# A two-layer decoder trunk: the second layer's input projection by seven products of block sums

## The chip, the cores and the metric

The kernel runs on one core of one Trainium2 chip. The metric is device time in microseconds (us). The time before is the median of three runs, 1857.2 us (1854.56 to 1858.99).

## The reference

The input x is 1024 tokens by 1024 features (h below). There are two layers. Each normalizes h, multiplies it with an input matrix, mixes, attends to a memory of 256 tokens, gates, and adds the product with an output matrix to h:

```python
hn = rms_norm(h, ln_g[i])
# layer 0: differential attention          # layer 1: causal pooling, windows 2, 4, 8, 16
proj = einsum('bsd,de->bse', hn, w_in)      # layer 0: 1024 x 7168, layer 1: 1024 x 4096
u, q_mem, gate = split(proj)                # layer 1: 1536 + 512 + 2048 columns
y = diff_attention(u, ...) or multiscale_pool(u, w_group, scale)
m = memory_attention(q_mem, mem_n, w_kv[i])
z = concatenate([y, m]) * silu(gate)
h = h + einsum('bse,ed->bsd', z, w_out[i])  # w_out: 2048 x 1024
```

After both layers h is normalized once more. `multiscale_pool` takes for each of four groups of 384 columns the mean of the last 2, 4, 8 or 16 tokens, subtracts the token itself, and multiplies with a 384 x 384 matrix.

## The kernel before, in words

Everything is kept with features on the 128 partitions and tokens along the free axis; the 1024 tokens are two halves of 512, worked on in the order 1, 0. A float32 product is made of three matmuls: each operand is split into a rounded part and a rest (a cast on ScalarE, and a subtract on VectorE or GpSimd), and `mm3` (L118) issues high x high, high x rest, rest x high. A tile of 128 output features for one half of the tokens is 8 such triples, one for each 128 input features (`project`, L204): 24 matmuls of 128 x 512.

The activations of a layer are split once, before normalization: `new_hidden` (L500) makes `hh` and `hl` from h times the gain. The row scale of the normalization is not known yet then. `row_means` and `row_spread` (L526, L532) make it, and each projected tile is multiplied by it when it is read from its PSUM bank, with the table `rsb` (L605, L625, L817, L1143).

TensorE's order is written by hand. Jobs are put in a list by `plan` (L971); `run_jobs` (L164) issues the loads of the next job (weights over the SP queue, then their split) before it runs the present one, and yields after each triple or so ("a step"). Attention and memory units play their own matmuls in between at given step counts (`play`, L747; `mem_units`, L703, with a list of starts). On the other engines the order comes from a planner with a priority by place in the program. PSUM has two banks of the tag "pj" for projections, two "t", three "s" and one "o".

The stages: attention of layer 0 with its projections; memory keys and values of both layers, and eight units of memory attention for layer 0 (`other_layers`, L1202), the last of which play into the next stage; the output projection of layer 0 (`out_jobs`, L1232), here called out0; the input projection of layer 1 with the layer's memory attention, the pooling and the group products, here the mixing stage; the output projection of layer 1 (out1).

out0 goes half by half in three rounds of 2, 4 and 2 output tiles. A round reads all 16 z tiles of its half from DRAM again: a chunk is one 512 KB weight tile with four z tiles (rounds 0 and 2) or two (round 1), 24 matmuls each way. `operand` (L1250) loads z into a raw tile `zf` (`nf` = 5 of them), casts into `zr` (`nz` = 6) and subtracts. `finish` (L1305) adds the residual to a finished tile, squares it, stores h to DRAM, and calls `new_hidden`. The row means of half 1 are taken after the first chunk of half 0, the spread after the third.

In the mixing stage, `projection_pair` (L181) runs two query tiles for half 1 while the row scale of half 0 is made; each further `projection` (L172) loads a weight tile of 512 KB, splits it, and runs both halves. `pooled_evac` (L1131) makes the sliding sums on GpSimd by doubling (L1155), subtracts the token and splits. `group_job` (L1175) runs one of a group's three output tiles in two "pj" banks, 9 matmuls a half, and multiplies with scale and gate (L1191). Groups go 0, 1, 2, 3. Layer 1's z tiles 12 to 15 are read first by out1, then 0 to 11.

## Time and profile before

| what | value |
|---|---|
| median of three runs | 1857.2 us (1854.56 to 1858.99) |
| profiled execution, own time | 1851.84 us |
| its span, first to last instruction | 1850.1 us |
| TensorE busy | 1778.2 us (96%), 8670 matmuls |
| VectorE, ScalarE, GpSimd busy | 66%, 49%, 39% |
| granted TensorE clock, mean | 0.989 |

A row of the waits reads: engine, tile and line that waited, what it waited for, us in total, times, longest. A row of a group of instructions reads: line, engine, operation, tiles, shapes, count, busy us, mean ns, and idle time ahead of them. In a row of one line's instructions three numbers behind the count are the shortest, median and longest duration in ns. A matmul's row has its start and a modelled duration; matmuls overlap, so the distance of two starts is what one costs.

### The profile page before, as it was taken

Reading aid. Unit: us, or ns where it says so; the run is one execution under the profiler, and the core shown is the slowest. Engines: PE = TensorE matmul, PEld = TensorE weight load, DVE = VectorE, ACT = ScalarE, POOL = GpSimd, SP = SyncE. Lnnn points to the kernel's source line nnn. Section 1 sums busy time; section 2 is a strip of 40 time slices with the busy share of each in tenths; the row PEclk is TensorE's granted clock in tenths of the full one; section 3 lists DMA queues with packets and bytes.
Section 4 is the critical chain, followed back from the end, with each engine's and each line's share of the span. In section 5 each row is a group of like instructions: output and inputs, shape, how many; then the busy total and the mean of one; then the engine's idle time right before and its main releaser. Section 6 shows DMA issues by size and latency. Waiting matters only on the chain. (4 is left out here: it accounts for less than half of the span.)

```text
span 1850.1 us, 24825 instructions
## 1 busy us (share of the span) xinstructions
PE 1778.2 (96%) x8670; PEld 1479.3 (80%) x8670; DVE 1223.2 (66%) x2446; ACT 899.7 (49%) x1649; POOL 724.1 (39%) x618
## 2 busy tenths in 40 slices
PE   6899999999999999999999999999999999999997
PEld 5788888888888888888787877778887777878885
DVE  7778788888889888876557777635453435444413
ACT  6667657657657756743256555533321111124522
POOL 4434344444344434433254343432332444513452
PEclk9999999999999999999999999999999999999998
DMA  5001111111111111112454778632213122155542
GB/s 184 27 31 58 46 42 51 46 47 51 41 52 52 40 53 46 58 58 69 169 184 172 246 258 277 216 106 86 92 37 96 47 73 77 56 161 200 172 148 97
DMA packets 80956, 186.04 MB, mean 101 GB/s; under 512 B 9120, under 2 KB 17024, under 8 KB 80832
## 3 DMA queue, kind: packets, MB, share of 16 engines
q1 hardware_dynamic: 79440, 182.04, 29.5%
q10 hardware_dynamic: 1296, 2.17, 0.3%
q8 instruction: 68, 1.11, 0.3%
q14 instruction: 56, 0.46, 0.1%
q0 software_dynamic: 96, 0.26, 0.1%
HBM read 152.67 MB, written 31.77 MB: 100 GB/s over the span
## 5 line engine op out<-in xcount | busy, mean ns | idle before, releaser
L865 ACT ACTIVATE e<-e,st 128x640 f32<-128x640 f32 (+4 forms) x192 | 148.2, 773 | 109.9 <-DVE st L856 108.8
L115 POOL TENSOR_TENSOR wl_o<-wf_o,wh_o 128x384 fp32r<-128x384 f32 x64 | 97.5, 1523 | 216.0 <-ACT wh_o L112 205.7
L877 POOL TENSOR_SCALAR e<-e,st 128x640 f32<-128x640 f32 (+4 forms) x96 | 76.3, 795 | 198.0 <-DVE st L876 115.5
L1267 DVE TENSOR_TENSOR zr<-zf,zr 128x512 fp32r<-128x512 f32 x132 | 114.5, 886 | 27.0 <-ACT zr L1266 26.7
L115 DVE TENSOR_TENSOR wl_o<-wf_o,wh_o 128x640 fp32r<-128x640 f32 x64 | 58.2, 909 | 110.5 <-ACT wh_o L112 104.7
L112 ACT CAST wh_o<-wf_o 128x1024 fp32r<-128x1024 f32 x64 | 67.2, 1049 | 115.7 <-PE ob L122 70.9
L905 ACT CAST wth<-wt 128x512 fp32r<-128x512 f32 (+2 forms) x168 | 72.4, 431 | 103.5 <-PE wt L902 73.8
L856 DVE CUSTOM_DVE_ANT_0 e<-s,mask 128x512 f32<-128x512 f32 (+2 forms) x192 | 109.3, 580 | 12.3 <-PE s L851 10.8
L1266 ACT CAST zr<-zf 128x512 fp32r<-128x512 f32 x132 | 80.8, 618 | 67.2 <-DMA zf<-z 32.9
L121 PE MATMUL ga<-hh,wh_ga 128*128 128x512 f32 x256 | 104.0, 406 | 3.5 <-DVE mqf L625 3.5
L121 PE MATMUL pga<-hh,wh_pga 128*128 128x512 f32 x256 | 100.5, 392 | 6.5 <-DVE pz L1191 4.6
L123 PE MATMUL ga<-hh,wl_ga 128*128 128x512 f32 x256 | 101.4, 396 | 0.0
L122 PE MATMUL ga<-hl,wh_ga 128*128 128x512 f32 x256 | 101.1, 395 | 0.0
L122 PE MATMUL ob<-zr,wh_o 128*128 128x512 f32 x256 | 100.3, 392 | 0.0
L121 PE MATMUL ob<-zr,wh_o 128*128 128x512 f32 x256 | 100.3, 392 | 0.0
L123 PE MATMUL ob<-zr,wl_o 128*128 128x512 f32 x256 | 100.3, 392 | 0.0
L122 PE MATMUL pga<-hl,wh_pga 128*128 128x512 f32 x256 | 99.8, 390 | 0.0
L123 PE MATMUL pga<-hh,wl_pga 128*128 128x512 f32 x256 | 99.7, 389 | 0.0
L851 PE MATMUL s<-kb,qa 128*128 128x512 f32 (+2 forms) x288 | 98.5, 349 | 0.9 <-DVE kb L803 0.9
L851 PE MATMUL s<-kb,qlo 128*128 128x512 f32 (+2 forms) x288 | 98.4, 349 | 0.0
L121 PE MATMUL k<-hh,wh_k 128*128 128x512 f32 x192 | 79.2, 412 | 8.5 <-ACT wh_k L112 8.5
L906 DVE TENSOR_TENSOR wtl<-wt,wth 128x512 fp32r<-128x512 f32 (+2 forms) x168 | 82.7, 492 | 6.0 <-ACT wth L905 4.8
(285 smaller groups left out, 5547.6 us busy)
## 6 DMA issues: line engine op xcount, KB each, us to landing
zf<-z SPq DMA_DIRECT2D x132, 256.0 KB, 3.8
wf_o<-in_w_out SPq DMA_DIRECT2D x64, 512.0 KB, 3.4
wf_ga<-in_w_in SPq DMA_DIRECT2D x16, 512.0 KB
wf_pga<-in_w_in SPq DMA_DIRECT2D x16, 512.0 KB, 4.4
wf_q<-in_w_in SPq DMA_DIRECT2D x12, 512.0 KB, 3.1
wf_v<-in_w_in SPq DMA_DIRECT2D x12, 512.0 KB, 3.8
z<-rs SPq DMA_DIRECT2D x24, 256.0 KB, 3.2
z<-z SPq DMA_DIRECT2D x24, 256.0 KB, 2.0
```

The costliest lines, as they stand in the source:

```text
L115: eng.tensor_tensor(wl[:, c], wf[:, c], wh[:, c].bitcast(F32), op=ALU.subtract)
L121: nc.tensor.matmul(out, sh, mh, start=first, stop=False)
L122: nc.tensor.matmul(out, sh, ml, start=False, stop=False)
L123: nc.tensor.matmul(out, sl, mh, start=False, stop=last)
L851: nc.tensor.matmul(sc[m][:, w], q[half][part][:, m, qs], k[kh][:, m, w], start=(part == 0), stop=(part == 1),)
L856: nc.vector.tensor_tensor_reduce(out=es[m][:, lo:hi], in0=sc[m][:, : hi - lo], in1=self.mask[:, S - n + lo : S - n + hi], scale=1.0, scala ...
L865: nc.scalar.activation(es[m][:, :n], es[m][:, :n], AF.Exp, bias=least[m], scale=-1.0, accum_out=st[:, 2, m : m + 1],)
L877: nc.gpsimd.tensor_scalar(es[1][:, :n], es[1][:, :n], st[:, 3, 1:2], 1.0, op0=ALU.mult, op1=ALU.mult)
L905: nc.scalar.copy(wh[:, lo:hi], t[:, lo:hi])
L906: nc.vector.tensor_tensor(wl[:, lo:hi], t[:, lo:hi], wh[:, lo:hi].bitcast(F32), op=ALU.subtract)
L1266: nc.scalar.copy(z[:, 0, :], zf)
L1267: nc.vector.tensor_tensor(z[:, 1, :], zf, z[:, 0, :].bitcast(F32), op=ALU.subtract)
```

## The change

The projection of layer 1 is done in blocks of halves. The input features are cut in two (block rows of the weights: a[:, k0], a[:, k1] and b[:, k0], b[:, k1] for a pair of output tiles a, b), and so are the tokens (X11, X21 for half 1, X12, X22 for half 0). Two output tiles for two halves are 8 block products; seven products of sums and differences of blocks give the same (Winograd's form), each of 4 triples, that is 12 matmuls. Its parts:

- The activations are normalized first: `finish` of layer 0 keeps h in SBUF in place of splitting it. When a half's row scale is spread, `scale_hidden` multiplies the 8 tiles by gain and scale on VectorE. `blocks_first` splits half 1 (inside out0's half 0, after the third chunk); `blocks_second` makes the four sums T1 to T4 and splits them and X22, after out0. Evacuations need no scale any more.
- `product` loads a pair's two weight tiles, makes S1, S2, S3 and the difference in place on VectorE, splits the block in a box (`split_box`), and runs 12 matmuls. Boxes are prepared four entries ahead (`entry`), raw tiles up to four more. `done` combines products on VectorE from their banks; products 4 and 3 add up in the banks of 7 and 5.
- The first four pairs (memory query and its gate) run products 1 and 2, which need half 1 alone, one pair after the other; row means and spread of half 0 stand behind the first and the second of them. Their loads of the first tile are made twice.
- The groups go 3, 2, 1, 0, with all six output tiles of a group in six banks ("t", "t", "s", "s", "s", "o"), one input tile after the other; w_group is stored in another order.
- The sliding sums go to VectorE from the second doubling on; buffers of the pooling shrink.
- The memory attention of layer 0 ends before out0 starts (starts 94 to 138 in place of 100 to 150); layer 1's units get other starts and single buffers.
- SBUF for the blocks comes from smaller buffers: in out0 `nf` 5 to 3, `nz` 6 to 5, one square tile; mask and rope tables live with the attention, `rsb` up to the end of layer 0's memory attention.

```diff
-        self.projection_pair([mq1(0), mq1(1)], lambda: means0(0), lambda: spread0(0))
-        self.mark("out0")
...
+        firsts = [self.pair(mq1(m), gate1(NH + m)) for m in range(MH)]
+        for i, p in enumerate(firsts):
+            self.product(p, 1)
+            self.product(p, 2)
+            if i == 0:
+                self.between(lambda: means0(0))
+            if i == 1:
+                self.between(lambda: spread0(0))
+        self.mark("out0")
+        for p in firsts:
+            for n in (6, 7, 5, 4, 3):
+                self.product(p, n)
...
+        def pairs(a, b):
+            p = self.pair(a, b)
+            for n in (1, 6, 2, 7, 5, 4, 3):
+                self.product(p, n)
+
+        for gi in (3, 2, 1, 0):
+            t = 3 * gi
+            pairs(u1(t), u1(t + 1))
...
+            pairs(gate1(t), u1(t + 2))
+            self.group(gi, 0)
+            pairs(gate1(t + 1), gate1(t + 2))
+            self.group(gi, 1)
+            self.group(gi, 2)
...
+        def prep(box):
+            a, b = (p["a0"], None) if early else (p["a"], p["b"])
+            if n == 6:
...
+                nc.vector.tensor_tensor(p["s1"], b[:, k0], b[:, k1], op=ALU.add)
+                nc.vector.tensor_tensor(p["s2"], p["s1"], a[:, k0], op=ALU.subtract)
+            if n == 7:
+                nc.vector.tensor_tensor(a[:, k0], a[:, k0], b[:, k0], op=ALU.subtract)
+            if n == 3:
+                nc.vector.tensor_tensor(p["s2"], a[:, k1], p["s2"], op=ALU.subtract)
...
+            self.split_box(box, f, HALF, nc.vector if n in (6, 3, 5) else nc.gpsimd)
...
+        def done(out):
+            if n == 1:
+                keep("p1", out)
+            elif n == 2:
+                evac0(1, out, None)
+            elif n == 6:
+                keep("u2", out, p["p1"])
+            elif n == 7:
+                keep("u3", out, p["u2"])
+            elif n == 5:
+                evac1(0, out, p["u3"])
+            elif n == 4:
+                evac1(1, out, p["u2"])
+            else:
+                evac0(0, out, p["u2"])
...
+    def scale_hidden(self, half, bc):
+        g = self.ln_g[1]
+        for d in self.h_order(half):
+            f = self.hid[half, d]
+            self.nc.vector.scalar_tensor_tensor(
+                f, f, g[:, d : d + 1], bc, op0=ALU.mult, op1=ALU.mult
+            )
+            yield d, f
...
+    def blocks_first(self, bc):
+        nc = self.nc
+        for d, f in self.scale_hidden(1, bc):
+            name, i = ("11", d) if d < 4 else ("21", d - 4)
+            self.split_block(name, i, f, 2 * d, 2 * d + 1, (nc.vector, nc.gpsimd)[d % 2])
+
+    def blocks_second(self, bc):
...
+            nc.vector.tensor_tensor(x11, x12, x11, op=ALU.subtract)
+            nc.vector.tensor_tensor(t2, x22, x11, op=ALU.subtract)
+            self.split_block("t2", i, t2, 16 + 2 * i, 17 + 2 * i, (nc.gpsimd, nc.vector)[i % 2])
+            nc.gpsimd.tensor_tensor(x21, x21, t2, op=ALU.subtract)
+            nc.gpsimd.tensor_tensor(x12, x22, x12, op=ALU.subtract)
...
-                nc.gpsimd.tensor_tensor(
+                (nc.gpsimd if sh == 1 else nc.vector).tensor_tensor(
...
-        nf, nz = ((5, 6), (4, 20))[layer]
+        nf, nz = ((3, 5), (4, 20))[layer]
...
             if layer == 0:
                 nc.sync.dma_start(self.h_dram[d][:, cols], h)
-                self.new_hidden(half, d, h, self.ln_g[1])
...
-                self.keep_spread(half)
+                bc = self.opool.tile([P, HALF], F32, tag="bc", name=f"bc{half}")
+                (self.blocks_second, self.blocks_first)[half](self.keep_spread(half, bc))
```

More of the change, by code (lines that the diff above doesn't have):

```diff
@@ L80, in build @@
             self.stream = self.run_jobs()
-            self.attention_layer()
+            with tc.tile_pool(name="scale", bufs=1, reuse_waits="tile") as pool:
+                self.rsb = pool.tile([P, S], F32, name="rsb")
+                self.attention_layer()
+                self.memory_layer()
             self.other_layers()
@@ L628, in mem_query_evac, with mem_query @@
         return evac
-    def mem_query(self, pool, layer, m, half):
+    def mem_query(self, pool, layer, m, half, bufs):
         nc = self.nc
@@ L701, in mem_value, with mem_units @@
         nc.tensor.matmul(o, kv[:, 0, c], wl, start=False, stop=(j == 1))
-    def mem_units(self, pool, layer, gates, starts):
+    def mem_units(self, pool, layer, gates, starts, bufs=2):
         nc = self.nc
@@ new lines, in pair, with entry, load @@
+    def pair(self, first, second):
+        return {"specs": (first, second)}
+    def entry(self, prep, run, fetch=lambda: None):
+        n = len(self.entries)
+        self.entries.append((prep, fetch))
+        boxes = {}
+        def load():
+            while self.ready < min(n + 4, len(self.entries)):
+                i = self.ready
+                self.ready += 1
+                for j in range(i, min(i + 4, len(self.entries))):
+                    self.entries[j][1]()
+                pool, tag = (
+                    (self.wpool, "wh"), (self.wpool, "wl"), (self.spool, "wb")
+                )[i // 2 % 3]
+                box = pool.tile(
+                    [P, 2, HALF], F32R, tag=tag, **({"bufs": 2} if tag == "wb" else {}),
+                    name=f"box{i}",
+                )
+                self.entries[i][0](box)
+                self.box[i] = box
+            return self.box.pop(n)
+        self.jobs.append((load, run))
@@ new lines, in land, with mem_query_keep, evac @@
+    def land(self, t, bank, more):
+        if more is None:
+            self.nc.scalar.copy(t, bank)
+        else:
+            self.nc.vector.tensor_tensor(t, bank, more, op=ALU.add)
+    def mem_query_keep(self, m):
+        def evac(half, bank, more):
+            f = self.epool.tile([P, HALF], F32, tag="ev", bufs=6, name=f"mqf1{m}{half}")
+            self.land(f, bank, more)
+            self.nc.sync.dma_start(self.mq_dram[1][m][:, half * HALF : (half + 1) * HALF], f)
+        return evac
@@ new lines, in gate_keep, with evac @@
+    def gate_keep(self, t):
+        nc = self.nc
+        def evac(half, bank, more):
+            pool, bufs = (self.mpool, 2) if t >= NH else (self.xpool, 3)
+            g = pool.tile([P, HALF], F32, tag=f"gate{half}", bufs=bufs, name=f"gap{t}{half}")
+            th = pool.tile([P, HALF], F32, tag="tanh", name=f"tanhp{t}{half}")
+            if more is not None:
+                self.land(g, bank, more)
+            x = bank if more is None else g
+            nc.scalar.activation(th, x, AF.Tanh, scale=0.5)
+            nc.vector.scalar_tensor_tensor(g, th, 1.0, x, op0=ALU.add, op1=ALU.mult)
+            self.gates[1][t][half] = g
+        return evac
@@ new lines, in slot, with split_block @@
+    def slot(self, j, name, dtype=F32R):
+        if j < 32:
+            half, d, part = 1 - j // 16, j % 16 // 2, "hl"[j % 2]
+            return self.hpool.tile([P, HALF], dtype, tag=f"h{part}{half}{d}", name=name)
+        return self.h2pool.tile([P, HALF], dtype, tag=f"n{j - 32}", name=name)
+    def split_block(self, name, i, f, hi, lo, by):
+        h = self.slot(hi, f"x{name}h{i}")
+        l = self.slot(lo, f"x{name}l{i}")
+        self.nc.scalar.copy(h, f)
+        by.tensor_tensor(l, f, h.bitcast(F32), op=ALU.subtract)
+        self.X.setdefault(name, {})[i] = (h, l)
@@ L1313, in finish @@
                 nc.sync.dma_start(r, a["x"][half, :, d, :])
-                h = pool.tile([P, HALF], F32, tag="hn", bufs=2, name=f"hn{nm}")
+                if half == 0 and d >= 4:
+                    h = pool.tile([P, HALF], F32, tag=f"hk{d}", name=f"hn{nm}")
+                else:
+                    h = self.slot(32 + (d if half else 8 + d), f"hn{nm}", F32)
+                self.hid[half, d] = h
             else:
```

298 lines of the change are left out of this document (185 added, 113 removed).

## The prediction

> **What bounds the kernel now.** I read the page first, then the stretches of the second half, TensorE's waits there, and its instructions one by one.
>
> ```profile
> span 1850.1 us, 24825 instructions
> PE 1778.2 (96%) x8670; PEld 1479.3 (80%) x8670; DVE 1223.2 (66%) x2446; ACT 899.7 (49%) x1649; POOL 724.1 (39%) x618
> ```
>
> ```profile
> core 0: us, PE busy (x) PEld busy (x) DVE busy (x) ACT busy (x) POOL busy (x), PEclk, DMA share, GB/s
> 1010.00:1202.00 192.00, 186.72 (x808) 150.56 (x807) 138.47 (x170) 104.73 (x160) 69.07 (x48) 0.99 0.72 243
> 1202.00:1322.00 120.00, 116.68 (x571) 96.64 (x570) 55.88 (x95) 42.43 (x101) 34.87 (x36) 0.99 0.31 105
> 1322.00:1653.00 331.00, 322.43 (x1423) 263.78 (x1422) 150.74 (x174) 65.70 (x90) 129.52 (x73) 1.00 0.21 68
> ```
>
> TensorE is the bound. The first stretch is the first layer's output projection (out0), the second the start of the second layer's input projection with the memory attention, the third the rest of it with the groups. In the second and third, where the change works, VectorE is busy under half and DMA under a third; out0 is the tight one: DMA 0.72, VectorE 138 of 192.
>
> ```profile
> PE pga L121 <- DVE pz L1191: 4.6, 6, 1.4
> PE ms_h L246 <- POOL ssq L524: 2.4, 1, 2.4
> PE oc L123 <- DVE wl_o L115: 2.3, 2, 1.2
> PE u L121 <- DVE pz L1191: 2.0, 3, 0.7
> PE pga L121 <- DVE pool L1166: 1.9, 1, 1.9
> ```
>
> Columns: who waited for whom, total us, times, longest. From 1010 to 1655 us these are TensorE's largest waits, so nearly all of that stretch is matmuls one behind the other, and their pitch is the price of one:
>
> ```profile
> 1202.09 0.39 PE L121 MATMUL pmq<-hh,wh_pmq 128*128 128x512 f32 x1
> ...
> 1207.31 0.39 PE L123 MATMUL pmq<-hh,wl_pmq 128*128 128x512 f32 x1
> ```
>
> 24 matmuls, first and last start: (1207.31 - 1202.09) / 23 = 0.227 us. The 0.39 in the rows is start to modelled end; they overlap.
>
> **The change, part by part.** *Products.* Now: 32 output tiles x 2 halves x 8 blocks x 3 matmuls = 1536. After: 16 pairs x 7 products x 4 blocks x 3 = 1344. 192 matmuls fewer x 0.227 = **-43.6 us**. The groups keep 216.
>
> *Group banks.* A group job takes a "pj" bank, and the next product waits for its result to be read: the three rows ending at L1191 and L1166, 8.5 us in 10 waits. They count from the modelled end, so 0.39 - 0.227 = 0.16 more each: **-10.1**. After, a group has six banks of the other tags. The new products keep the two "pj" banks: taken strictly in turn, product 7 gets the bank that product 2 has just left and waits about 0.8 for its reading; the other was read a product earlier (2.7 us). I take the free one, at nothing; without that cover it is 12 pairs x 0.8 = 9.6.
>
> *Memory attention of layer 0 moved ahead of out0.* Its first scores come 6 steps earlier (first start 94, not 100).
>
> ```profile
> 935.77 0.69 ACT L456 ACTIVATE mvf<-mv,rsym 128x512 f32<-128x512 f32 x1 [0.70 <-PE mv L123]
> 944.29 0.62 ACT L650 CAST mkvr<-mkv 128x512 fp32r<-128x512 f32 x1 [1.79 <-DMA mkv<-mv]
> ```
>
> ```profile
> PE ms L121 <- ACT mkvr L650: 0.6, 1, 0.6
> ```
>
> The values leave at 935.77, go through DRAM on the SP queue, and are split at 944.29; the scores already wait for them. Six steps x 3 x 0.227 = 4.1 us of matmuls stood in between, and nothing else in TensorE's written order replaces them: **+4.1** (0 to 5).
>
> *out0's buffers.* Raw tiles "zf" go from 5 to 3, split tiles "zr" from 6 to 5. Rounds 0 and 2 use four z tiles a chunk of 24 matmuls, one each 24 x 0.227 / 4 = 1.36 us; round 1 half as many.
>
> ```profile
> L1267 DVE TENSOR_TENSOR zr<-zf,zr 128x512 fp32r<-128x512 f32 x90 | 82.6, 934 | 10.5 <-ACT zr L1266 10.3
> L1266 ACT CAST zr<-zf 128x512 fp32r<-128x512 f32 x90 | 55.2, 618 | 46.9 <-PE ob L123 16.9 <-DMA zf<-z 13.1 <-PE oa L123 12.4
> ```
>
> ```profile
> SPq L1265 <- DVE zr L1267: 42.1, 58, 3.1
> ```
>
> ```profile
> L1267 DVE TENSOR_TENSOR zr<-zf,zr x132: 677/692/1791, 996.7 to 1744.0; 128x512 fp32r<-128x512 f32 x132
> ```
>
> ```profile
> DMA to landing us min/median/max: 2.6/3.8/4.9
> ```
>
> The last row is for the z loads: a slot is taken from issue until its subtract ends, 3.8 + 0.62 + 0.93 = 5.35 us (2.6 + 0.62 + 0.68 = 3.9 at best, 4.9 + 0.62 + 1.79 = 7.3 at worst), and SP waits for slots even with five (58 times). Five must turn in 6.8 us, three in 4.09: 1.26 late a turn. Behind a waiting z load on SP stand the next weights, residuals and stored hidden tiles. A round has 16/3 = 5.33 turns; 5 split and 3 raw tiles may be ahead when it starts, which covers half: 2.67 turns x 1.26 x 4 tight rounds = **+13.4**. Bounds: 0 at the best turn; 3.2 x 5.33 x 4 = 68 at the worst with no head start.
>
> *Splitting of the hidden tiles leaves out0* (per finished tile one ScalarE scale and one VectorE op), so the two waits of 2.3 on "wl_o" just behind four finishes should go: **-2.3** (0 to -2.3).
>
> *Blocks of half 1*, inside out0's last half: 8 scalings and 4 subtracts on VectorE, 8 casts, 4 subtracts on GpSimd, ahead of the conversions of the chunk after next.
>
> ```profile
> L524 POOL TENSOR_TENSOR ssq<-ssq,ssq x25: 1284/1299/1875, 1040.3 to 1814.7; 128x512 f32<-128x512 f32 x25
> ```
>
> VectorE 12 x 0.69 = 8.3, GpSimd 4 x 1.3 = 5.2; one chunk of 24 x 0.227 = 5.45 covers. Over by 2.9 if VectorE alone counts, 8.1 if the two take turns, 0 if it slips into idle time: **+3**.
>
> *Blocks of half 0*, the hinge. After the scale is spread TensorE has products 1 and 2 of pairs three and four: 48 x 0.227 = 10.9, and product 6 needs its last block 9 matmuls later: 12.9. By then VectorE has 8 scalings, 8 subtracts and 2 splits, 18 x 0.69 = 12.4, after a 0.6 copy and before a cast of 0.6: 13.6, late by 0.7. GpSimd's 10 subtracts (10 x 1.3 = 13.0) come in between; if the two exclude each other it is 26.6, late by 13.7. Which is it?
>
> ```profile
> L607 DVE SCALAR_TENSOR_TENSOR gap<-tanhp,gap x32: 678/716/2881, 1236.9 to 1642.6; 128x512 f32<-128x512 f32 x32
> L605 DVE TENSOR_TENSOR gap<-pga,rsb x32: 676/691/692, 1234.6 to 1641.2; 128x512 f32<-128x512 f32 x32
> ```
>
> An op with both inputs in SBUF (L607) takes up to 2.9 us, one with an input from a PSUM bank (L605) never over 0.692: half of the new work is exposed. I take **+8**, nearer the middle, since not every op meets a GpSimd one. The remaining 16 block splits have the 60 matmuls of the first pair, 13.6 us, and fit (12 x 0.69 + 2 x 1.3). [...]
>
> *VectorE in the mixing stage.* A pair has 7 products, 84 x 0.227 = 19.1 us, and 12 VectorE ops (4 sums, 3 splits, 5 evacuations), 8.3 us; an evacuation now has one product, 2.7 us, where it had half a projection, 5.4. The sliding sums go largely from GpSimd to VectorE.
>
> ```profile
> L1160 DVE SCALAR_TENSOR_TENSOR pool<-ws,u x12: 1212/1224/3411, 1341.0 to 1619.7; 128x1024 f32<-128x1024 f32 x12
> L1191 DVE SCALAR_TENSOR_TENSOR pz<-grp,pscale,gap x24: 731/735/751, 1386.4 to 1649.3; 128x512 f32<-128x512 f32 x24
> L1155 POOL TENSOR_TENSOR ws<-u x12: 1917/1918/2913, 1338.4 to 1607.6; 128x1039 f32<-128x1039 f32 x12
> ```
>
> The window-16 group: 3 x 8.3 + 6 gates x 0.72 + 15 wide ops x 1.22 + 6 x 0.735 + edges 1 = 52.9 of 3 x 19.1 + 54 x 0.227 = 69.6. GpSimd: 12 x 1.3 + 3 x 1.92 + 3 group splits at about 1 = 24.4. Fully exclusive, 77.3, over by 7.7; the window-8 group 3.7 less work, over by 4.1, the others about 0.4 and 0. Bounds 0 and 12.2: **+6**.
>
> *Order of groups reversed*: z tiles 0 to 2 are stored last and read in out1's second chunk, 5.45 us later; store and load by the rows above take about 2 x 3.8 + 1.3. Their first use is covered within some 1 to 3: **+1**.
>
> Weights: as many bytes as before and four 512 KB loads more, at a DMA share of 0.31; hidden by that idle share (without it 4.4 us each).
>
> Sum: -43.6 - 10.1 + 4.1 + 13.4 - 2.3 + 3 + 8 + 6 + 1 = **-20.5**. The profiled execution took 1851.84 (span 1850.1), giving 1831.3; the runs' median is 5.4 above it, 1857.2, giving **1836.7**, forecast 1837.
>
> **Rivals.** *B, the cover is better:* the head start fills the tight rounds (+2), the transition costs 3, the mixing 3, the rest nothing: -43.6 - 10.1 + 4.1 - 2.3 + 8 = -43.9, 1813. For it: five slots rarely starve TensorE now; against: SP waits 58 times for a slot.
> *C, slower:* three raw slots decide out0. Without head start each of 21.3 turns counts; with a turn of 6.3 (middle of 5.35 and 7.3) that is 2.2 x 21.3 = 47 in place of 13.4: 1837 + 34 = 1870. It outweighs the gain from a turn of 4.09 + (13.4 + 20.5) / 21.3 = 5.68 on. For it: weights queue behind the z loads on SP, DMA 0.72; against: VectorE's load there falls.
> *D, VectorE and GpSimd in turns everywhere:* 13.7, 12.2 and 8.1 in place of 8, 6 and 3: +17, 1854, hardly any change; the exposed SBUF row (2.9) speaks for it, its median against. [...]
> *That it saves no matmuls* I rule out by the loop counts.
>
> **How the numbers follow.** Forecast 0.54 (own range 1822 to 1850), B 0.20, C 0.16, D 0.10. 0.2% is 3.7 us, about what a measurement of this kernel can tell from no change: 1853.5 to 1860.9 is "same". Faster: 0.53 + 0.19 + 0.04 = 0.76; same: 0.01 + 0.01 + 0.05 = 0.07; slower the rest, 0.17. The range leaves out the best of B and the far half of C: 1808 to 1866.
>
> **What would show it.** Right: 1344 matmuls of pitch 0.227 in the projection; no waits on L1191's successor; SP waiting longer for zf slots, and TensorE waiting for zr in rounds 0 and 2 of out0, some 3 us a round; one wait of about 8 us ahead of the first product 6; VectorE over 70% in the window-16 group. Wrong: out0 longer than 225 us (C), or as short as 185 (B); the transition under 2 us; TensorE waiting at evacuations in every pair.

## The result, and the profile after

The changed kernel takes 1899.95 us, median of four runs (1894.44 to 1904.2), beside 1855.88 us for the kernel before on the same chip: a ratio of 1.0236, 95% interval 1.0202 to 1.027. It is slower by 44 us where 20.5 us less were forecast. Its profiled execution took 1894.44 us. The page's first rows after:

```profile
span 1892.7 us, 24833 instructions
PE 1760.5 (93%) x8478; PEld 1452.4 (77%) x8478; DVE 1338.9 (71%) x2608; ACT 951.6 (50%) x1765; POOL 746.0 (39%) x660
```

8670 - 8478 = 192 matmuls are gone, as counted; VectorE has 115.7 us more work. The stretches that answer to the three shown of before: out0 first, then the start of the mixing stage cut finer, then the rest of it.

```profile
core 0: us, PE busy (x) PEld busy (x) DVE busy (x) ACT busy (x) POOL busy (x), PEclk, DMA share, GB/s
1020.00:1230.00 210.00, 187.51 (x786) 146.63 (x785) 134.07 (x164) 100.44 (x150) 77.67 (x51) 0.98 0.69 228
1230.00:1256.00 26.00, 22.21 (x101) 17.05 (x99) 16.44 (x32) 10.61 (x19) 12.30 (x8) 1.00 0.38 132
1256.00:1280.00 24.00, 10.69 (x22) 6.76 (x22) 22.20 (x20) 11.33 (x21) 21.57 (x12) 0.58 0.17 55
1280.00:1306.00 26.00, 20.74 (x76) 15.67 (x76) 18.69 (x28) 9.54 (x22) 8.02 (x10) 0.73 0.20 62
1306.00:1381.00 75.00, 67.77 (x332) 53.90 (x331) 54.90 (x88) 33.98 (x88) 24.18 (x31) 0.98 0.27 88
1381.00:1690.00 309.00, 290.62 (x1261) 235.63 (x1260) 206.86 (x264) 96.92 (x161) 108.80 (x85) 0.98 0.21 70
```

The third row is the centre of the case. From 1256 to 1280 us TensorE runs 22 matmuls, which need 22 x 0.227 = 5 us; VectorE is busy 22.2 of 24, GpSimd 21.6, and the granted clock falls to 0.58. TensorE's waits, by stage (memory, out0, the first 76 us of mixing, the rest of mixing, out1):

```profile
PE ms L125 <- ACT mkvr L645: 4.5, 1, 4.5
```

```profile
PE oa L126 <- DVE zr L1512: 12.1, 8, 6.5
PE oc L125 <- ACT zr L1511: 4.2, 3, 2.6
```

```profile
PE pmq_pga15x L125 <- ACT p1pmq_pga L1169: 6.6, 1, 6.6
PE pmq_pga12y L126 <- POOL xt2l L1236: 6.3, 2, 4.3
PE pmq_pga12y L126 <- DVE xt2l L1236: 2.9, 1, 2.9
PE pmq_pga12y L125 <- ACT xt2h L1235: 2.2, 1, 2.2
```

```profile
PE grp L125 <- ACT ph L1395: 6.9, 1, 6.9
PE mt L681 <- POOL me L672: 3.9, 4, 1.5
PE pga_u2z L125 <- DVE u2pga_u L1171: 1.9, 1, 1.9
```

```profile
PE oa L125 <- ACT zr L1511: 8.1, 1, 8.1
```

Before, no single wait in these stages was over 2.7 us; the longest was one of these two, at out1's start:

```profile
PE oa L121 <- ACT zr L1266: 4.0, 2, 2.7
```

"Transition" is here the stretch from the first product of the mixing stage to the end of the first pair, in which the blocks of half 0 are made. A part of this work in order of time, first a row of GpSimd, then the rows of VectorE:

```profile
1269.27 1.70 POOL L1236 TENSOR_TENSOR xt2l<-t,xt2h 128x512 fp32r<-128x512 f32 x1
```

```profile
1268.10 1.75 DVE L1236 TENSOR_TENSOR xt2l<-t,xt2h 128x512 fp32r<-128x512 f32 x1
1269.77 1.75 DVE L1142 TENSOR_TENSOR wf_pmq_pga13a<-wf_pmq_pga13a,wf_pmq_pga13b 128x512 f32<-128x512 f32 x1
1271.44 1.76 DVE L1236 TENSOR_TENSOR xt3l<-hn,xt3h 128x512 fp32r<-128x512 f32 x1
1273.12 0.68 DVE L1107 TENSOR_TENSOR box<-s2pmq_pga,box 128x512 fp32r<-128x512 f32 x1
```

While both engines have work with two SBUF inputs here, an operation takes 1.70 to 1.76 us; an operation of VectorE alone takes 0.68. And the queue holds not only the blocks: the next weight boxes (`box`, `wf_pmq_pga13a`) stand between them.

Where the 42.6 us between the two spans lie, by the first start of each stage's first product on TensorE in the two traces:

| stage | before | after | difference |
|---|---|---|---|
| up to the memory keys | 912.4 | 913.5 | +1.1 |
| memory, to out0's first product | 97.7 | 106.7 | +9.0 |
| out0 | 191.9 | 209.8 | +17.9 |
| mixing | 447.0 | 459.5 | +12.5 |
| out1, to the end | 201.0 | 203.2 | +2.2 |

(20 matmuls, 4.5 us, have moved from out0's stretch into the memory stage: 804 and 572 before, 784 and 592 after.) In the mixing stage, taking from each matmul's distance to the next its pitch in undisturbed stretches, 20.3 us were lost before and 75.9 after: 35.7 up to the end of the first pair, 14.3 from there to the first u tile, 25.8 in the rest. So -43.6 for the 192 matmuls and +55.6 of new losses make the +12.

### The profile page after: what moved, and what is told of

Its sections match the earlier page's. It is cut to its first block, busy times and chain, and to the rows that moved or that the text cites. A ratio compares the mean times of both kernels' runs of the same rounds, so it can differ in the third digit from the quotient of the medians.

```text
span 1892.7 us, 24833 instructions
## 1 busy us (share of the span) xinstructions
PE 1760.5 (93%) x8478; PEld 1452.4 (77%) x8478; DVE 1338.9 (71%) x2608; ACT 951.6 (50%) x1765; POOL 746.0 (39%) x660
## 5 line engine op out<-in xcount | busy, mean ns | idle before, releaser
L1512 DVE TENSOR_TENSOR zr<-zf,zr 128x512 fp32r<-128x512 f32 x132 | 109.8, 851 | 60.5 <-ACT zr L1511 59.8
L875 DVE SCALAR_TENSOR_TENSOR e<-e,st,e 128x640 f32<-128x640 f32 (+4 forms) x96 | 77.9, 811 | 9.9 <-POOL e L872 9.2
L897 PE MATMUL wt<-cst,e 128*128 128x128 f32 x432 | 69.9, 276 | 15.0 <-DVE e L875 12.6
L125 PE MATMUL v<-hh,wh_v 128*128 128x512 f32 x192 | 79.5, 414 | 0.0
```

What stands on the lines that cost most here:

```text
L125: nc.tensor.matmul(out, sh, mh, start=first, stop=False, skip_group_check=more)
L875: nc.vector.scalar_tensor_tensor(es[0][:, :n], es[0][:, :n], st[:, 3, 0:1], es[1][:, :n], op0=ALU.mult, op1=ALU.add)
L1512: nc.vector.tensor_tensor(z[:, 1, :], zf, z[:, 0, :].bitcast(F32), op=ALU.subtract)
```

## The experiments

Totals confuse here: with another arrangement of memory the stages ahead of the memory keys take up to 6 us more, and the memory stage up to 9. So each experiment is read in the stage that it edits, from one profiled execution. Stages that a run does not edit differ too: the transition, 75.8 us in the changed kernel, reads 75.8 to 78.4 in e1, e2, e12 and e14, and 79.6 in e6, which moves its tiles. A difference of 3 us there shows nothing by itself.

| run | median, us | ratio to before (95%) | memory | out0 | transition | mixing | out1 |
|---|---|---|---|---|---|---|---|
| the change | 1899.95 | 1.0236 (1.0202 to 1.027) | 106.7 | 209.8 | 75.8 | 459.5 | 203.2 |
| e1 | 1892.36 | 1.0195 (1.018 to 1.021) | 115.9 | 190.7 | 75.8 | 461.7 | 203.7 |
| e2 | 1892.5 | 1.0201 (1.0179 to 1.0223) | 106.4 | 208.8 | 76.7 | 453.9 | 206.2 |
| e3 | 1889.8 | 1.0173 (1.0157 to 1.0189) | 115.9 | 215.2 | 46.4 | 434.0 | 204.1 |
| e4 | 1900.18 | 1.0235 (1.0206 to 1.0263) | 107.1 | 211.5 | 73.6 | 460.3 | 204.1 |
| e5 | 1903.15 | 1.0242 (1.0227 to 1.0258) | 106.9 | 212.9 | 73.0 | 461.5 | 204.3 |
| e6 | 1880.38 | 1.0117 (1.01 to 1.0134) | 106.4 | 186.7 | 79.6 | 467.9 | 204.2 |
| e7 | 1896.12 | 1.0206 (1.0188 to 1.0224) | 102.4 | 205.1 | 81.4 | 461.1 | 203.9 |
| e8 | 1875.23 | 1.0095 (1.0077 to 1.0112) | 105.9 | 191.8 | 74.5 | 454.4 | 206.0 |
| e9 | 1891.17 | 1.0179 (1.0156 to 1.0201) | 106.6 | 210.9 | 65.0 | 453.6 | 203.6 |
| e10 | 1902.36 | 1.0247 (1.0226 to 1.0268) | 106.1 | 209.2 | 72.5 | 457.2 | 206.6 |
| e11 | 1878.09 | 1.012 (1.0102 to 1.0138) | 102.8 | 189.3 | | 463.5 | 206.6 |
| e12 | 1904.0 | 1.0256 (1.0238 to 1.0273) | 106.5 | 211.3 | 76.0 | 461.9 | 205.3 |
| e13 | 1853.56 | 0.9984 (0.9969 to 0.9998) | 104.4 | 189.9 | | 438.6 | 204.3 |
| e14 | 1898.63 | 1.0226 (1.0198 to 1.0253) | 105.5 | 207.6 | 78.4 | 466.1 | 199.9 |
| e15 | 1849.38 | 0.9967 (0.9949 to 0.9985) | 101.9 | 189.5 | | 436.9 | 200.5 |
| e16 | 1840.85 | 0.9913 (0.9878 to 0.9948) | 102.4 | 189.5 | | 428.6 | 201.1 |

### out0: the raw slots (e1, e6)

```diff
-        nf, nz = ((3, 5), (4, 20))[layer]
+        nf, nz = ((5, 6), (4, 20))[layer]
...
+                if layer == 0:
+                    self.nzf = getattr(self, "nzf", -1) + 1
+                    zf = self.h2pool.tile([P, HALF], F32, tag=f"n{16 + self.nzf % nf}", name=f"zf{nm}")
...
```

> The changed kernel with out0's buffers as before (five raw z tiles, taken from block tiles that stand empty until the blocks of half 0 are made, and six split ones). Theory Z, that three raw slots starve out0: out0 (209.8 us in the changed kernel, 191.9 before) loses about 14 us, time about 1885. Rival, that out0 is longer because of the blocks of half 1 and their meetings on VectorE and GpSimd: out0 stays above 203, time 1894 or more.

Measured: out0 209.8 to 190.7, but the memory stage grew by 9.2: out0's first products waited 10 us. The first loads of z went out at 1028.42, just behind the store of the memory attention's last result (1028.05), where the changed kernel has them from 1002.11 on. That the raw tiles lie in room which the memory attention still held fits this and was not tested by itself. e6 has five raw tiles in the old place and leaves the split tiles at five:

```diff
-        nf, nz = ((3, 5), (4, 20))[layer]
+        nf, nz = ((5, 5), (4, 20))[layer]
...
-            t2 = self.opool.tile([P, HALF], F32, tag="tt", bufs=2, name=f"t2_{i}")
+            t2 = self.opool.tile([P, HALF], F32, tag="zf", bufs=5, name=f"t2_{i}")
```

> out0's raw tiles zf go from 3 back to 5, in the same place of memory, and the split tiles zr stay at 5; the room comes from the two tiles of T2, which now lie in the ring of zf. Theory Z (the raw slots set the loss of out0): out0 falls from 209.8 us to 191 to 195, without the late start of the run with five raw tiles elsewhere (its wait of 10 us); whole 1882 to 1887. Rival R (the fifth and sixth split tile count as well): out0 only falls to about 200; whole about 1890.

Measured: out0 186.7, 23.1 us less, better than the run expected. TensorE's waits of e6 in out0:

```profile
PE ob L126 <- DVE zr L1512: 3.7, 1, 3.7
PE ms_h L250 <- POOL ssq L518: 1.5, 1, 1.5
```

Of the 12.1 and 4.2 next to nothing is left; the wait of 6.5 us, which came behind VectorE's eight scalings of half 1, is now one of 3.7 (the row on `ob`). With the 4.5 us of moved matmuls out0 takes 191.2, beside 191.9 before: with five raw tiles out0 loses nothing, and a sixth split tile is not needed for that. But the mixing stage grew by 8.4 us, 6.8 of it in one wait for the memory attention's query: the first loads of that attention go out 54.5 us after the stage's first product where the changed kernel has them after 37.3. So the total shows 19.6 of the 23.1.

### The transition: order, engine, or amount of work (e3, e4, e5, e9, e10)

e3 leaves out the making of the half-0 blocks (the products take half-1 blocks in their place):

```diff
     def blocks_second(self, bc):
...
+        for name, other in (("t2", "11"), ("t3", "21"), ("t1", "11"), ("t4", "21"), ("22", "11")):
+            self.X[name] = self.X[other]
```

> The changed kernel without the making of the blocks of half 0: no scaling of half 0, no sums T1 to T4 and no splits; the products that need them read the blocks of half 1, so all matmuls stay and the output is not the reference's. It prices the whole transition. Theory T (the blocks block VectorE, GpSimd and ScalarE for 30 us): 25 to 32 us less, time about 1871. Rival (the mixing stage is slow all along, for want of VectorE): 8 to 14 us less, as the forecast priced it.

Measured: the transition falls by 29.4 us and mixing by 25.5. VectorE then has little to do there, and the clock stays whole:

```profile
1264.00:1276.00 12.00, 10.61 (x50) 8.29 (x49) 5.53 (x7) 5.68 (x11) 2.66 (x4) 1.00 0.45 141
```

The total shows only 10 of it: under the other arrangement the memory keys began 6.2 us later, the memory stage took 9.2 more (out0's first products waited 9.6, as in e1) and out0 5.4 more. e4 takes the block work from GpSimd and gives it to VectorE:

```diff
-            self.split_block("t2", i, t2, 16 + 2 * i, 17 + 2 * i, (nc.gpsimd, nc.vector)[i % 2])
-            nc.gpsimd.tensor_tensor(x21, x21, t2, op=ALU.subtract)
-            nc.gpsimd.tensor_tensor(x12, x22, x12, op=ALU.subtract)
+            self.split_block("t2", i, t2, 16 + 2 * i, 17 + 2 * i, nc.vector)
+            nc.vector.tensor_tensor(x21, x21, t2, op=ALU.subtract)
+            nc.vector.tensor_tensor(x12, x22, x12, op=ALU.subtract)
...
-                "t4", i, h[1, 4 + i], 44 + i, 40 + i, (nc.gpsimd, nc.vector)[i % 2]
+                "t4", i, h[1, 4 + i], 44 + i, 40 + i, nc.vector
```

> The changed kernel with all 12 GpSimd operations of the blocks of half 0 done on VectorE. VectorE then has 44 operations of 0.69, 30 us, but meets no GpSimd operation. Theory L (the two engines hold each other up: single operations of 1.75 and 7 us in the trace): the transition gets 8 to 12 us shorter, time about 1890. Rival W (the number of operations sets it): no gain or up to 8 us loss.

```profile
PE pmq_pga12y L126 <- DVE xt2l L1236: 8.9, 4, 5.8
PE ms L125 <- ACT mq L631: 8.3, 1, 8.3
PE pmq_pga12y L125 <- ACT xt2h L1235: 3.0, 1, 3.0
PE pmq_pga15x L125 <- ACT p1pmq_pga L1169: 0.7, 1, 0.7
```

The 6.6 us behind GpSimd's slow subtract went, and the same time came back as waits for VectorE and, later, for the memory attention's query. The blocks themselves were done sooner: the last one 47.8 us after the stage's first product, 55.5 in the changed kernel. But the loads of the memory attention went out only after 49.8 us, not 37.3, and the 8.3 us wait is for them. e5 shortens what stands ahead of product 6:

```diff
+                if half == 0 and d >= 4:
+                    x12, g = self.hid[0, d - 4], self.ln_g[1]
+                    nc.scalar.activation(x12, x12, AF.Copy, scale=g[:, d - 4 : d - 3])
+                    nc.vector.scalar_tensor_tensor(
+                        x12, h, g[:, d : d + 1], x12, op0=ALU.mult, op1=ALU.subtract
+                    )
...
+            nc.vector.tensor_tensor(h[0, i], h[0, i], bc, op=ALU.mult)
+            nc.vector.tensor_tensor(t, h[0, i], h[1, i], op=ALU.add)
+            t2.append(t)
+            self.split_block("t2", i, t, 16 + 2 * i, 17 + 2 * i, nc.vector)
```

> Only the making of the half-0 blocks is rewritten; every other part is the changed kernel's. The block T3 without its row scale (x22 g22 - x12 g12) is made as out0 finishes its tiles; after the spread T3 is one multiplication by the row scale, read from its PSUM bank, and T2 = T3 + x11 one addition, so that 2 VectorE operations stand ahead of each block of product 6 where 4 stood (two scalings, two subtractions). Theory T (the number of operations ahead of product 6 sets the transition): VectorE has 8 x 0.7 + 4 splits x 0.7 = 8.4 us under 10.9 us of products; the waits on the blocks of product 6 (4.33 + 2.19 + 1.96 + 2.85) go, and the stretch from the first product to the end of the first pair falls from 75.8 us to about 62, the whole by 13 to 20 us: 1880 to 1887. Rival Q (ScalarE's written order: the copy of p1 of the fourth pair stands behind a block's cast): the 6.57 us wait of a product 2 stays, and the stretch stays over 68 us.

Measured 73.0, not 62. The same waits as in e10 below came. e10 is e5 with the right of way for T2 (the cut shows e10 against e5):

```diff
+            with self.tc.high_priority(offset=SOON):
                 nc.vector.tensor_tensor(h[0, i], h[0, i], bc, op=ALU.mult)
                 nc.vector.tensor_tensor(t, h[0, i], h[1, i], op=ALU.add)
                 self.split_block("t2", i, t, 16 + 2 * i, 17 + 2 * i, nc.vector)
```

> As the run with T3 made before the row scale, but VectorE and ScalarE take the multiplication, the addition and the split of T2 before everything else that is ready. In that run T2's low halves were made from 1271 to 1278, behind the subtracts of T3, although they are written ahead of them. Theory T (order): the waits on T2 of 2.58 and 0.64 go and product 2's wait of 3.78 too, nothing takes their place, and the stretch to the end of the first pair falls from 73.0 us to under 66. Theory V (VectorE's total work): T2's waits go, but T3's, T1's or T4's blocks or the memory attention's query (a wait of 4.65 there) are late by as much; the stretch stays at 70 to 75.

```profile
PE ms L125 <- ACT mq L631: 4.6, 1, 4.6
PE pmq_pga15x L125 <- ACT p1pmq_pga L1169: 3.8, 1, 3.8
PE pmq_pga12y L126 <- DVE xt2l L1236: 3.3, 4, 1.8
```

72.5 us, 3 less than in the changed kernel, about what unedited runs differ by. In e5 and e10 too the last block was done sooner (after 49.6 and 49.5 us), and the next wait, 4.6 us for the memory attention's query, stands right behind it. e9 changes nothing ahead of T2 and leaves out 16 low halves behind it:

```diff
...
+        if name in ("t3", "t1", "t4", "22"):
+            l = self.X["11"][i][1]
+        else:
+            l = self.slot(lo, f"x{name}l{i}")
+            by.tensor_tensor(l, f, h.bitcast(F32), op=ALU.subtract)
```

> Leaves out the 16 subtracts that make the low halves of the blocks T3, T1, T4 and 22 (products take another block's low half there); nothing ahead of T2 changes, all sums and all high halves are made. In the changed kernel VectorE is busy 22.2 of the 24 us from 1256 to 1280. Theory V (all of VectorE's and GpSimd's work between the spread and the last block is the bound, whatever its order): 14 of the 16 are VectorE's, 14 x 0.7 to 1.75 = 10 to 24 us; the stretch from the first product to the end of the first pair falls from 75.8 us to between 52 and 66, out of 46.4 without any block work. Rival T (only what stands ahead of product 6 counts): the waits of 6.57 and 4.33 + 2.19 + 1.96 + 2.85 stay, and the stretch stays over 72.

```profile
PE pmq_pga15x L125 <- ACT p1pmq_pga L1169: 5.4, 1, 5.4
PE pmq_pga12y L126 <- POOL xt2l L1239: 4.7, 2, 3.7
```

65.0 us, just inside what the theory of VectorE's total work gave, and outside the other: work that is written behind T2 delays T2. The 6.6 us wait stayed for the most part (5.4), as the rival had it, and the waits of product 6 (6.3, 2.9 and 2.2) are down to 4.7 together. The two amounts agree: 44 operations less (8 scalings, 16 sums, 20 low halves; e3) save 29.4 us, 0.67 each, and 16 less save 10.8, 0.68 each; with the scatter of 3 us the second can be 0.5 to 0.9. So less work between the spread and the last block shortens the transition. Another order or engine (e4, e5, e10) did not, though the blocks were then done 6 to 8 us sooner: the memory attention's query came next. No run has such an order together with a later memory attention and the same products, so what order alone is worth stays open.

### Waits of order (e2, e7, e8)

```diff
...
-            self.group(gi, 0)
+            self.group(gi, 1)
             pairs(gate1(t + 1), gate1(t + 2))
-            self.group(gi, 1)
+            self.group(gi, 0)
             self.group(gi, 2)
...
```

> The changed kernel with each group's input tiles multiplied in the order 1, 0, 2 in place of 0, 1, 2. In the trace a pair's second tile is complete before its first (products 5 and 4 come ahead of 3), so the group's first product waits for the tile that is pooled last. Theory O (wrong order): the 6.9 us wait ahead of the window-16 group and the ones of 1 to 3 us in the others go, time 10 us less (about 1890). Rival (VectorE is simply full there, 53 us of work in 70): the wait moves to the next group product, time within 3 us of 1900.

Measured: the wait of 6.9 us ahead of the group is gone and mixing is 5.6 us shorter. A pair finishes its second u tile before its first (products 5 and 4 come ahead of 3), so the first group began with the tile that came last. e7 adds three more changes of order:

```diff
...
-                self.mpool, 0, self.gates[0][NH:], [94, 101, 108, 114, 120, 126, 132, 138]
+                self.mpool, 0, self.gates[0][NH:], [100, 106, 112, 117, 123, 128, 133, 138]
...
-        korder = list(range(16)) if layer == 0 else list(range(12, 16)) + list(range(12))
+        korder = list(range(16)) if layer == 0 else [12, 13, 14, 15, 9, 10, 11, 6, 7, 8, 3, 4, 5, 0, 1, 2]
...
+        for p in firsts[:2]:
+            self.product(p, 1)
+        self.between(lambda: means0(0))
+        for p in firsts[:2]:
+            self.product(p, 2)
...
```

> Four changes of order, no operation more or less, each seen in its own stage: the scores of the first memory attention start 6 steps later (as before the change), product 1 of two pairs is issued ahead of product 2 of both (so that each copy of p1 has a product as cover), the middle block of each group goes first (as in the run with that order), and out1 takes its z tiles in the order in which the groups store them. Expected, if each wait is one of order: 4.46 us ahead of the first scores falls under 1; the three waits of 0.68 on p1 go, and the one of 6.57 falls; 6.87 ahead of group 3 goes; the wait of 8.06 at out1's start falls to 4 or less. Together 15 to 20 us: 1880 to 1885. Rival: a later operand is only just behind (the blocks of product 6, the last stored z tile), so the waits move and half of it is seen: about 1890.

Measured: the wait of the memory scores went (that stage 106.7 to 102.4), the group's went; the copies' 0.7 and 6.6 went, but 3.9 us on the row means and 8.7 on the first block of T2 took their place; and out1 still waited 8.1 us:

```profile
PE oa L125 <- ACT zr L1513: 8.1, 1, 8.1
```

So the order in which z tiles are stored is not what delays out1. e8 has e5, e6 and e7 together:

> The three others in one kernel (T2's four tiles in the ring of zf). If the losses are separate, they add: 1900 - 16 - 16 - 17 = 1851, within 0.5% of the kernel before. If they share a cause (one queue or engine that is late everywhere), the sum of gains falls to about half: 1875.

It reached 1875, the figure given for losses that share a cause, but that was reckoned from gains that did not come. The totals that the three runs did reach lie 19.6 and 3.8 us under the changed kernel and 3.2 over it, which adds up to 1879.8; so e8 does not tell the two theories apart. By stage, out0 (191.8) and the group kept most of their gains, the transition (74.5) has none to speak of.

### The two banks (e12)

```diff
...
-                p[life] = self.pj(f"{nm}{life}")
+                p[life] = (self.sb if n == 7 and p.get("wide") else self.pj)(f"{nm}{life}")
```

> Product 7 of the pairs that hold a u (but for the first such pair) takes a bank of another tag, free between the groups, in place of the one of the two that product 6 has just left; nothing else changes. Theory P (the two banks, taken strictly in turn, cost the waits of 1.75 to 1.9 ahead of product 7 on VectorE's reading of product 6): the three waits in the pairs with u8, u5 and u2 go and the groups' stretch falls from 308.2 us by 5 to 6; whole about 1894. Rival (VectorE is behind in these pairs, so the next reading, of product 5 or of u, waits for as long): the stretch falls by under 2 us.

```profile
PE pga_u8z L125 <- DVE u3pga_u L1172: 4.3, 1, 4.3
```

The waits on u2 (product 6's reading) went, and waits on u3 (product 7's reading), ahead of product 4, came: 4.3, 1.8 and 1.3 us in the same three pairs. From the first u to out1 it took 309.2 us, 308.2 in the changed kernel. With another bank VectorE's readings are just as late: they are the cause, not the bank.

### Out1's start (e14)

In the changed kernel all six results of a group come in its last 18 matmuls. VectorE's reading of the last group, in order of time:

```profile
1686.26 1.40 DVE L1431 SCALAR_TENSOR_TENSOR pz<-grp,pscale,gap 128x512 f32<-128x512 f32 x2
...
1692.06 1.41 DVE L1431 SCALAR_TENSOR_TENSOR pz<-grp,pscale,gap 128x512 f32<-128x512 f32 x2 [1.51 <-DMA z<-pz]
1695.78 1.41 DVE L1431 SCALAR_TENSOR_TENSOR pz<-grp,pscale,gap 128x512 f32<-128x512 f32 x2 [2.31 <-DMA z<-pz]
```

They go two by two, each two behind the stores of the two before.

```diff
-                        z = self.xpool.tile([P, HALF], F32, tag="z", bufs=2, name=f"pz{t}{half}")
+                        z = self.epool.tile([P, HALF], F32, tag="ev", bufs=6, name=f"pz{t}{half}")
```

> The changed kernel, but the group's results go to the ring of six evacuation tiles in place of their own two. In the changed kernel all six results of a group come within its last 18 matmuls (4.1 us), and at the end the readings at 1692.06 and 1695.78 wait for the stores of the earlier ones (ended by a DMA of z). Theory S (two z tiles set the start of out1, behind which its z loads stand on SP): the wait of 8.06 us at out1's start falls to 4 or less, as before the change, out1 from 203.2 to about 199; whole 1895. Rival (its raw tiles' room, free only when the mixing's tiles are): the wait stays over 7.

```profile
PE oa L125 <- ACT zr L1511: 4.5, 1, 4.5
```

The wait fell by 3.6 and out1 to 199.9, under the 201.0 of before. The total fell by 1.3 only: the transition and the rest of the memory pairs took 6.2 us more in that run, ahead of anything that the edit touches, and why is open (from the first u on it is 308.6 beside 308.2).

### More cover in place of less work (e11, e13, e15, e16)

If the block work can't be made shorter, TensorE must have more to do meanwhile. e11 multiplies the four memory pairs plainly: half 1 needs blocks X11 and X21 alone, and half 0 is a0 X12 + a1 X22 = (a0 + a1) X22 - a0 T3. It holds the useful edits of above as well (five raw tiles, later scores, the group's order, T3 ahead of the row scale).

```diff
...
+    def plain(self, spec, half):
...
+                block = (("22", "t3"), ("11", "21"))[half][part]
...
+        for m in range(MH):
+            self.plain(mq1(m), 1)
...
+        for t in (NH, NH + 1):
+            self.plain(gate1(t), 1)
+        for m in range(MH):
+            if m > 1:
+                self.plain(gate1(NH + m), 1)
+            self.plain(mq1(m), 0)
+            self.plain(gate1(NH + m), 0)
```

> Gives the making of the blocks more cover in place of less work: the four memory pairs are multiplied in the plain way (8 block products: a0 x11 + a1 x21 and the same for b in half 1, (a0 + a1) 22 - a0 T3 and the same for b in half 0), 12 matmuls more for each pair, 48 in all, +10.9 us; after the spread 4 + 4 products (21.8 us) need only blocks of half 1, where 4 did, and T2, T1 and T4 are needed only by the first pair of sums, over 40 us later. With it come five raw tiles in out0, the later memory scores, the middle block of a group first, and T3 made before the row scale. Theory V: the some 29 us of the transition go; mixing 459.5 + 10.9 - 29 - 6 = 435 us, out0 187, memory stage 4 less: about 1848, under the kernel before by 0.3 to 0.8%. Rival (the block work is only pushed along and waits for the memory attention's queries and the conversions take its place): mixing 450 or more, 1862 to 1870.

Measured 1878.09: the products wait for no block any more, and one new wait took most of the gain. TensorE's waits, GpSimd and SP's queue in order of time:

```profile
PE ms L125 <- ACT mq L631: 23.9, 2, 22.7
```

```profile
1250.55 5.83 POOL L1284 TENSOR_TENSOR xt1l<-t,xt1h 128x512 fp32r<-128x512 f32 x2 [7.30 <-ACT xt1h L1283]
```

```profile
1255.18 0.33 SPq L638 DMA_DIRECT2D mkv<-mk  x1
...
1256.50 0.43 SPq L630 DMA_DIRECT2D mql<-mq  x1
```

The loads of the memory attention start as the first of the two `xt1l` of GpSimd ends (1255.16): their tiles take the room of out0's, and the raw blocks of T2 and T1 lie there until the last split. Block work that no product needs yet still holds what needs its room. e13 starts the memory attention later (against e11):

```diff
-                            self.mpool, 1, self.gates[1][NH:], [14, 42, 31, 62, 58, 82, 79, 104],
+                            self.mpool, 1, self.gates[1][NH:], [46, 58, 52, 69, 75, 88, 85, 104],
```

> The run with plain memory pairs, but the second layer's memory attention starts 32 steps of 3 matmuls (21.8 us) later and its eight units follow more closely. In that run the only large wait of the transition was the first scores': 22.69 us for the query's cast, and the loads of the query and the values were issued at 1255.18, when the last low half of T1 (whose raw block lies in the room of out0 that the memory attention's tiles take over) was done at 1255.16. Theory M (the block work still has to end before the memory attention gets its room; TensorE only lacks other work until then): the wait falls under 4 us, mixing from 463.5 to about 443, whole about 1857, the kernel before's time. Rival (the block work itself is slowed by the products that now run beside it): the wait stays over 12 us.

Measured: mixing 438.6 and the whole 1853.56, but one wait of 12.8 us stayed, on another tile. e15 adds e14's ring, and out1 gains 3.8 us, about as alone:

> The two others together, with the larger ring under the plain memory pairs: if both hold, 1857 - 5 = 1852, under the kernel before by 0.2%; if only the first, 1857; if neither, 1878.

```profile
PE pmq L125 <- DVE gap L1267: 12.8, 1, 12.8
```

```profile
1252.26 7.64 POOL L1284 TENSOR_TENSOR xt1l<-t,xt1h 128x512 fp32r<-128x512 f32 x2 [7.30 <-ACT xt1h L1283]
```

```profile
1258.70 0.69 DVE L1267 SCALAR_TENSOR_TENSOR gap<-tanhp,pga 128x512 f32<-128x512 f32 x1 [1.16 <-POOL xt1l L1284]
```

The gate's evacuation writes a tile in the same room and waits for the same split; TensorE waits for its bank. e16 gives the first two gates other banks (against e15):

```diff
         for t in (NH, NH + 1):
-            self.plain(gate1(t), 1)
+            self.plain(gate1(t), 1, self.sb)
...
```

> The run before it (plain memory pairs, later memory attention, larger ring for the groups' results) with one edit: the half-1 results of the first two gates go to two banks of another tag, which stand empty until the memory attention. In that run TensorE waits 12.82 us at 1246.24 for a bank: the gate's evacuation writes a tile in the room of T2, and waits for GpSimd's low half of T1, which took 6.41 us and ended at 1258.67. The blocks T3 and 22 that the next products need were done at 1245.51. Theory M (room, not work, is the last wait): the products of half 0 start at once, the wait falls under 3 us, mixing from 436.9 to about 426, whole about 1839, some 1% under the kernel before. Rival V (VectorE, busy 12.23 of those 14 us, is behind with the weight boxes too): the wait only changes its name and the whole stays at 1846 or more.

```profile
1211.00:1247.00 36.00, 34.14 (x159) 28.19 (x158) 26.40 (x42) 16.55 (x30) 27.23 (x14) 1.00 0.34 117
1247.00:1263.00 16.00, 13.78 (x58) 10.80 (x57) 15.69 (x18) 8.22 (x15) 7.25 (x7) 0.98 0.26 85
```

```profile
PE pmq L125 <- ACT mqf L1243: 1.9, 1, 1.9
```

The block work of e15, with VectorE as full (15.69 of 16 us), now lies under 13.78 us of products at a granted clock of 0.98, and the longest wait of the mixing stage is 1.9. GpSimd's two `xt1l` took 1.63 and 1.56 us here, where e15 has 6.41 and 1.27, so the shorter split may have its part in the gain beside the banks. The run takes 1840.85 us, a ratio of 0.9913 (0.9878 to 0.9948): 0.9% less time than the kernel before, with 8526 matmuls, 48 more than the changed one.

## Why the prediction was wrong

The forecast gave -20.5 to the span; it was +42.6. Term by term (the measured ones sum to 42.2):

| step, as the prediction put it | predicted | measured | by |
|---|---|---|---|
| products | -43.6 | -43.6 | 192 matmuls fewer |
| memory attention moved ahead | +4.1 | +4.5 | the wait on `mkvr`; gone in e7 |
| out0's buffers | +13.4 | +23.1 | e6 |
| hidden splitting, blocks of half 1 | +0.7 | -0.7 | the remainder: e6's out0 with the 4.5 us moved, 186.7 + 4.5 - 191.9 |
| blocks of half 0, the hinge | +8 | +29.4 | e3 |
| group banks and VectorE in mixing | -4.1 | +26.2 | the remainder: 75.9 - 29.4 lost, 20.3 before |
| order of groups reversed | +1 | +2.2 | out1's stage; the cause was another |
| ahead of the memory keys | 0 | +1.1 | not studied |

*The hinge* failed first. Its step "By then VectorE has 8 scalings, 8 subtracts and 2 splits, 18 x 0.69 = 12.4" named the work of T2 alone. In the trace of the changed kernel, from the copy of the scale (1245.24) to the end of T2's last split (1282.92), VectorE ran 37 operations and was busy 35.2 of 37.7 us: those 18, 12 low halves of the other blocks, which are written behind T2 but ran ahead of its last split, and 7 operations for the next weight boxes. From 1261 to 1282, beside GpSimd's, they took about 1.75 us instead of 0.69; beside the subtract of 7.06 us (1252.58) they kept 0.68. The step "The remaining 16 block splits have the 60 matmuls of the first pair, 13.6 us, and fit" failed with it: most of these splits ran ahead of T2's last one, and the sum counted the blocks alone. Whether the two engines exclude each other, on which the bounds of 0.7 and 13.7 were built, no run shows by itself, and it was not the main question: e4 took GpSimd out and moved the transition by 2 us, e9 took work away and moved 10.8, e3 29.4, and e16 gave the work cover.

*VectorE in the mixing stage* and *group banks* failed together. The old waits on `pz` and `pool` did vanish, but what replaced them was looked for only in the sum of VectorE's busy time over a whole group. New were single waits inside a group: 6.9 us because the group began with the tile that is finished last (e2: -5.6), 1.75 to 1.9 in each of the three other groups because VectorE reads late (e12: another bank doesn't help), 2.7 in copies of p1 (four times 0.7, left in e3). The prediction's point on the bank ("I take the free one, at nothing") had the bank right, the one that product 6 left, and the price wrong: in the pair with u8 VectorE began to read it 4.1 us after product 6's last matmul had started (1494.11 and 1498.24), later than the product of 2.7 us that should cover it. About half of the 26.2 is not separated by a run; 3.9 us of that are four waits of the memory attention for GpSimd (`me`), where before there was one of under 1 us.

*out0's buffers* was right in its mechanism and too small: 23.1 is between the forecast's 13.4, with a head start for half of the turns, and rival C's 47, with none and a slower turn. Which of the two was off was not separated.

*Order of groups reversed* was near in size, by luck, and wrong in its cause: not the order of the z tiles (e7) but two tiles for six results that come at once (e14).

The rivals: C's slots cost half of its price. D's condition, VectorE and GpSimd in turns, agrees with parts of the transition (from 1261 to 1273 us, for one, operations of both took 1.7 to 1.78 us), but was priced at 17 us, on bounds that left out the other work. None of the rivals had the forecast's hinge and its mixing stage both short of VectorE's time: each sum of VectorE's work left out what another part gave it.

Of the signs named, the matmuls and their pitch, the vanished waits on `pz` and longer waits for raw slots on SP came as said; out0 (209.8) lay between the marks of B and C. The one wait of 8 us ahead of the first product 6 came as four of 11.4 together, with one of 6.6 ahead of a product 2; VectorE was busy 69% in the window-16 group, not over 70%. "TensorE waiting at evacuations", the sign of a wrong forecast, came in each group but not in each pair.

In the rows of 1.70 to 1.76 us the two engines start by turns, VectorE at 1268.10, 1269.77 and 1271.44, GpSimd at 1269.27 and again at 1270.93; the next operation of VectorE, at 1273.12 with GpSimd idle, takes 0.68. What makes the others longer the trace does not show.

By the trace's clock record the clock was at half for 10.2 us from 1256.3 and 23.9 us from 1269.9, which is the 0.58 and 0.73 of the windows. In these stretches 42 matmuls that waited for nothing lost 8.4 us against their usual distance, by the same count as above; that is about the clock's share of the 35.7, an estimate. In e3, without the waits, the clock there is 1.00. In e16 it is at half for 3.4 us from 1262.2, right behind a wait of 1.9 us, its longest there. What sets how long the clock stays at half no run shows.

## What to carry to other kernels

Where a change moves arithmetic into the moment between a row scale and the first product that needs it, add up everything that the elementwise engine has in its queue up to the last new block (weight preparation and evacuations too), price an operation by rows in which GpSimd has work beside it (here 1.75 us, not 0.69), and compare that sum with the products that don't need the new blocks. If it doesn't fit, another order may only bring the next wait forward, as here; more independent products there (here 48 matmuls more) covered it. Room counts as a dependency: a tile that takes over the place of a late block waits for it, though no data passes.

## What was not expected of the hardware

A GpSimd operation took ten times as long as a VectorE operation beside it. In the changed kernel one subtract of 128x512 took 7.06 us while VectorE ran a train of operations with two SBUF inputs at their usual 0.68; the three like it that follow took about 1.73:

```profile
1252.58 7.06 POOL L1270 TENSOR_TENSOR hn<-hn,hn 128x512 f32<-128x512 f32 x1 [5.87 <-DVE hn L1266]
...
1260.83 1.73 POOL L1270 TENSOR_TENSOR hn<-hn,hn 128x512 f32<-128x512 f32 x1
```

ScalarE's cast of its result stood ahead of the copy of p1 in ScalarE's order of work, and that made the 6.6 us wait of TensorE, four engines in one chain:

```profile
1259.67 0.62 ACT L1235 CAST xt3h<-hn 128x512 fp32r<-128x512 f32 x1 [5.92 <-POOL hn L1270]
1260.20 0.58 ACT L1169 COPY p1pmq_pga<-pmq_pga15x 128x512 f32<-128x512 f32 x1
```

In e13 and e15 the same happened with 6.41 us (in e15 the first of two operations, 7.64 us together in the row above), in e11 with 4.61. Why operations of both engines take 1.70 to 1.76 us at one time (1268 to 1273), and at another (1252.58 to 1259.6) those of VectorE 0.68 and GpSimd's one 7.06, was not settled.
